# Hard-max attention: a group's key chosen in five steps, and the next batch's key differences formed on GpSimd in eight pieces

## The chip, the cores and the metric

One core of one Trainium2 chip. The time is that of one execution on the device, in microseconds (us); a run that is called *fast* is one of the undisturbed state, and only fast runs of the same rounds are compared. The profile was taken of one execution of each kernel. Its engines are PE (TensorE), PEld (weight loads), DVE (VectorE), ACT (ScalarE), POOL (GpSimd) and SP (the queue that issues most stores).

## The reference

```python
B, Sq, Sk, D = 4, 4096, 4096, 128           # q, k, v: float32, random normal
logits = np.matmul(q, k.transpose(0, 2, 1))
best = np.argmax(logits, axis=-1)
return v[b_idx, best, :]                    # the value row of the best key, for each query
```

The output needs the exact best key of each query, but not the logits.

## The kernel before

There are 128 iterations, 32 for each batch; an iteration handles 128 queries. The kernel screens in fp16 and repairs with exact arithmetic the few rows where the screen could be wrong.

1. *Screen.* Keys are taken in groups of four. TensorE and ScalarE give, per group, an upper figure of its four logits, 1024 figures per query. VectorE folds them into a word (`fold`: figure in the upper half, group number counted down in the lower half) and MAX8 takes the best eight words (`top`).
2. *Pick within the group.* `gather` cuts the group number out of the best word, and GpSimd fetches the group's three key differences k1-k0, k2-k0, k3-k0 with an indirect DMA. `dots` multiplies them with the query and adds up on VectorE; every two iterations make one such set. `pick`, once for each chunk of eight iterations (four at the end, 18 chunks in all), takes the best of the four and counts how many keys are near it. A second indirect DMA on GpSimd fetches the value row.
3. *Next batch.* Keys and queries of the next batch are loaded by GpSimd-issued DMAs (iterations 2 to 17 of a batch), and `put_k` forms the key differences on VectorE, two operations per batch, and stores them to DRAM, where the gathers of the next batch read them.
4. *Flags.* Rows whose decision is close are computed exactly: once in the middle of the kernel, beside the rest, and once at the end.

```python
def put_k(b, h):                                   # iterations 9 and 13 of the batch before
    src = natk[b % 2][:, h].rearrange("p (g f) d -> p g f d", f=4)
    nc.vector.tensor_tensor(out=kd[:, h], in0=src[:, :, 1:4, :],
                            in1=src[:, :, 0:1, :].to_broadcast([P, 4, 3, P]), op=OP.subtract)
    nc.sync.dma_start(out=kb16[:, h], in_=kd[:, h]...)
# ...
def dots(c, x, m):                                 # m = 2 iterations' queries
    yield "until", lambda: ("kg", x) in done, 2    # two iterations after the gathers were issued
    nc.vector.tensor_tensor(out=prod, in0=kg, in1=natq..., op=OP.mult)         # 128x768 fp16
    nc.vector.tensor_tensor(out=p1, in0=prod[..., 0:64], in1=prod[..., 64:128], op=OP.add)
    nc.vector.tensor_tensor(out=p2, in0=p1[..., 0:32], in1=p1[..., 32:64], op=OP.add)
    nc.vector.tensor_reduce(out=d[...], in_=p2, axis=AX_X, op=OP.add)

def pick(c, t0, t1):                               # seven VectorE operations; d is 128 x n x 4
    mx   = max over the four of d
    near = (d + NEAR) >= mx
    CNT  = sum of near                             # over 1.5: the row is flagged
    lt   = d < mx
    sel  = lt * 2**20 + iotab[b]                   # iotab: 0..3, plus the batch's first row
    wi   = min of sel
    win  = 4 * cand + wi                           # the row of v
    for j in range(n):                             # later, one or two per iteration
        late_q.append(lambda: nc.gpsimd.indirect_dma_start(out=vr[:, j, :], in_=v_flat, in_offset=win[:, j]))
# ... the loop, cut to its order:
for it in range(T):
    load_part(...)                                 # GpSimd issues a DMA, iterations 2..17 of a batch
    screen(it); fold(it - 1)
    if it % NQT in (9, 13): put_k(it // NQT + 1, it % NQT // 13)
    step(it)                                       # one operation of dots, pick, flags
    top(it - 2); gathers(it - 3); step(it)
    issue(it)                                      # GpSimd: one key gather, one or two value gathers
```

(The operations of `pick` are written as formulas here; `...` marks cuts.) GpSimd executes in the order of the program, so where an operation stands among its gathers decides when it runs.

Of the kernel before, what the change touches and what calls it, by code (L numbers as in the profile page):

```python
# [7 lines left out]
FP32 = mybir.dt.float32  # L8
FP16 = mybir.dt.float16
BF16 = mybir.dt.bfloat16  # L10
U32 = mybir.dt.uint32
# [3 lines left out]
AX_X = mybir.AxisListType.X  # L15
OP = mybir.AluOpType
AF = mybir.ActivationFunctionType
IOA = bass.IndirectOffsetOnAxis
# [9 lines left out]
def kernel(ctx, tc, q, k, v, out):  # L28
    nc = tc.nc
    B, Sq, D = q.shape  # L30
    Sk = k.shape[1]
    P = 128
    NQT = Sq // P
    T = B * NQT
    NG = Sk // 4

    k4 = k.rearrange("b (g f) d -> (b g) (f d)", f=4)
    v_flat = v.rearrange("b s d -> (b s) d")
# [14 lines left out]
    rec = dr.tile([P * T, 8], U32, name="rec")  # L53
    k16 = [dr.tile([NG, 384], FP16, name=f"k16_{b}") for b in range(B)]
    kT = [bp.tile([P, Sk], FP16, name=f"kT{i}", tag=f"kT{i}") for i in range(2)]
# [12 lines left out]
    def put_k(b, h):  # L68
        if b >= B:
            return  # L70
        src = natk[b % 2][:, h].rearrange("p (g f) d -> p g f d", f=4)
        nc.vector.tensor_tensor(out=kd[:, h], in0=src[:, :, 1:4, :], in1=src[:, :, 0:1, :].to_broadcast([P, 4, 3, P]),
                                op=OP.subtract)
        kb16 = k16[b].rearrange("(h p n) d -> p h (n d)", p=P, n=4)
        nc.sync.dma_start(out=kb16[:, h], in_=kd[:, h].rearrange("p g f d -> p (g f d)"))

    def load_part(b, i):
# [32 lines left out]
    for W in W_t:  # L110
        nc.gpsimd.iota(out=W.bitcast(U16)[:, 0::2].rearrange("p (h m r) -> p h m r", h=2, m=4),
                       pattern=[[-NG // 2, 2], [-1, 4], [-4, P]], base=NG - 1, channel_multiplier=0)

# [5 lines left out]

    iotab = [iota(f"iotab{b}", 4, b * Sk) for b in range(B)]  # L120
    iota4 = iotab[0]
    iota_r = iota("iota_r", P, 1)
# [111 lines left out]
    def gather(c, t0, n):  # L234
        c0, c1 = chunks[c]
        if t0 == c0:
            cand_t[c] = sp.tile([P, c1 - c0], U32, tag=f"cand{c1 - c0}", name=f"cand_{c}", bufs=3)
        x = cand_t[c][:, t0 - c0:t0 - c0 + n]
        nc.vector.tensor_scalar(out=x, in0=TOP.bitcast(U32)[:, t0:t0 + n, 0], scalar1=NG - 1, scalar2=NG - 1,
                                op0=OP.bitwise_and, op1=OP.bitwise_xor)  # L240
        kg = rp.tile([P, n, 3, P], FP16, tag=f"kg{n}", name=f"kg_{t0}", bufs=8)
        assert len(kg_t) < 8
        kg_t[t0] = kg
        for j in range(n):
            near_q.append(lambda j=j: nc.gpsimd.indirect_dma_start(  # L245
                out=kg[:, j].rearrange("p f d -> p (f d)"), out_offset=None, in_=k16[t0 // NQT],
                in_offset=IOA(ap=x[:, j:j + 1], axis=0)))
        mark = lambda: done.add(("kg", t0))
        marks.add(mark)
        near_q.append(mark)  # L250
        start(dots(c, t0, n), "dots", c)
# [20 lines left out]
    def pick(c, t0, t1):  # L272
        n = t1 - t0
        b, qt = t0 // NQT, t0 % NQT
        d = D_t[c % 3][:, 0:n, :]
        yield "until", lambda: all(("dot", x) in done for x in range(t0, t1, 2)), 0
        cand = cand_t.pop(c)
        mx = sp.tile([P, n, 1], FP32, tag=f"mx{n}", name=f"mx_{c}")
        nc.vector.tensor_reduce(out=mx[:, :, 0], in_=d, axis=AX_X, op=OP.max)
        yield "dve",  # L280
        near = sp.tile([P, n, 4], FP32, tag=f"near{n}", name=f"near_{c}")
        nc.vector.scalar_tensor_tensor(out=near, in0=d, scalar=NEAR, in1=mx.to_broadcast([P, n, 4]),
                                       op0=OP.add, op1=OP.is_ge)
        yield "dve",
        nc.vector.tensor_reduce(out=CNT[:, t0:t1], in_=near, axis=AX_X, op=OP.add)
        done.add(("cnt", c))
        yield "cnt",
        lt = sp.tile([P, n, 4], FP32, tag=f"lt{n}", name=f"lt_{c}")
        nc.vector.tensor_tensor(out=lt, in0=d, in1=mx.to_broadcast([P, n, 4]), op=OP.is_lt)
        yield "dve",  # L290
        sel = sp.tile([P, n, 4], FP32, tag=f"sel{n}", name=f"sel_{c}")
        nc.vector.scalar_tensor_tensor(out=sel, in0=lt, scalar=float(1 << 20),
                                       in1=iotab[b].unsqueeze(1).to_broadcast([P, n, 4]), op0=OP.mult, op1=OP.add)
        yield "dve",
        wi = sp.tile([P, n], FP32, tag=f"wi{n}", name=f"wi_{c}")
        nc.vector.tensor_reduce(out=wi, in_=sel, axis=AX_X, op=OP.min)
        yield "dve",
        win = sp.tile([P, n], U32, tag=f"win{n}", name=f"win_{c}")
        nc.vector.scalar_tensor_tensor(out=win, in0=cand, scalar=4.0, in1=wi, op0=OP.mult, op1=OP.add)
        vr = rp.tile([P, n, P], FP32, tag=f"vr{n}", name=f"vr_{c}", bufs=3 if n == 8 else 4)  # L300
        for j in range(n):
            late_q.append(lambda j=j: nc.gpsimd.indirect_dma_start(out=vr[:, j, :], out_offset=None, in_=v_flat,  # L302
                                                                   in_offset=IOA(ap=win[:, j:j + 1], axis=0)))

        def store():
            nc.sync.dma_start(out=out[b].rearrange("(p t) d -> p t d", p=P)[:, qt:qt + n], in_=vr)
            done.add(("out", c))

        stores.add(store)
        late_q.append(store)  # L310
# [6 lines left out]
    def flag_segment(t0, t1, ready, stored):  # L317
# [8 lines left out]
        yield "dve", 0.17  # L326
        nc.vector.scalar_tensor_tensor(out=F, in0=CNT[:, t0:t1], scalar=1.5, in1=F, op0=OP.is_gt, op1=OP.max)
        yield "dve", 0.17
# [81 lines left out]
        def get(dst, src, idx, hi):  # L410
# [6 lines left out]
        bo = fp.tile([P, 1], U32, tag="bo", name=f"bo_{t0}")  # L417
        nc.vector.tensor_scalar(out=bo, in0=row, scalar1=Sq.bit_length() - 1, scalar2=NG.bit_length() - 1,
                                op0=OP.logical_shift_right, op1=OP.logical_shift_left)
        yield "dve", 0.17  # L420
        gi = fp.tile([P, 3], U32, tag="gi", name=f"gi_{t0}")
        nc.vector.tensor_scalar(out=gi, in0=FR[:, 0:3], scalar1=NG - 1, scalar2=NG - 1, op0=OP.bitwise_and, op1=OP.bitwise_xor)
        yield "dve", 0.17
# [3 lines left out]
        for r in range(3):  # L427
            get(FK[:, r, :], k4, gb[:, r:r + 1], B * NG)
        yield "until", lambda: not fast, 3
# [17 lines left out]
    def flags_last(t0, t1, win_last, late):  # L447
        S = t1 - t0
        H, F = LF["H"], LF["F"]
        nc.vector.scalar_tensor_tensor(out=F, in0=CNT[:, t0:t1], scalar=1.5, in1=F, op0=OP.is_gt, op1=OP.max)  # L450
        Ec = fp.tile([P, S], FP32, tag="Ec", name="Ec_e")
# [41 lines left out]
        def get(dst, src, idx, hi):  # L493
# [7 lines left out]
        bo = fp.tile([P, 1], U32, tag="bo", name="bo_e")  # L501
        nc.vector.tensor_scalar(out=bo, in0=row, scalar1=Sq.bit_length() - 1, scalar2=NG.bit_length() - 1,
                                op0=OP.logical_shift_right, op1=OP.logical_shift_left)
# [4 lines left out]
        gi = fp.tile([P, 3], U32, tag="gi", name="gi_e")  # L508
        nc.vector.tensor_scalar(out=gi, in0=FR[:, 0:3], scalar1=NG - 1, scalar2=NG - 1, op0=OP.bitwise_and, op1=OP.bitwise_xor)
        gb = fp.tile([P, 3], U32, tag="gb", name="gb_e")  # L510
        nc.vector.tensor_tensor(out=gb, in0=gi, in1=bo.to_broadcast([P, 3]), op=OP.add)
        for r in range(3):
            get(FK[:, r, :], k4, gb[:, r:r + 1], B * NG)
        tot = fp.tile([P, 3], FP32, tag="tot", name="tot_e")
# [18 lines left out]
    def exact(kk, qq, grp, R, name):  # L533
        d = fp.tile([P, R, 4], FP32, tag=f"xd{R}", name=f"xd_{name}")
        for r in range(R):
            for f in range(4):
# [4 lines left out]
        ix = fp.tile([P, R, 4], FP32, tag=f"xi{R}", name=f"xi_{name}")  # L541
        nc.vector.scalar_tensor_tensor(out=ix, in0=grp.unsqueeze(2).to_broadcast([P, R, 4]), scalar=4.0,
                                       in1=iota4.unsqueeze(1).to_broadcast([P, R, 4]), op0=OP.mult, op1=OP.add)
        yield "dve", 0.17
# [22 lines left out]
    def all_rows():  # L567
# [4 lines left out]
        with tc.If(left > 0):  # L572
            for b in range(B):
                with tc.For_i(0, NQT, 1) as t:
# [4 lines left out]
                    g8 = fp.tile([P, 8], U32, tag="ag", name=f"ag_{b}")  # L579
                    nc.vector.tensor_scalar(out=g8, in0=w8, scalar1=NG - 1, scalar2=(NG - 1) | (b * NG),  # L580
                                            op0=OP.bitwise_and, op1=OP.bitwise_xor)
                    kk = fp.tile([P, 8, 512], FP32, tag="ak", name=f"ak_{b}")
                    for r in range(8):
                        nc.gpsimd.indirect_dma_start(out=kk[:, r, :], out_offset=None, in_=k4,
                                                     in_offset=IOA(ap=g8[:, r:r + 1], axis=0))
# [92 lines left out]
    for it in range(T):  # L678
# [17 lines left out]
        if it >= 1:  # L696
            fold(it - 1)
        if it % NQT in (9, 13):
            put_k(it // NQT + 1, it % NQT // 13)
        step(it)  # L700
        if it >= 2:
            top(it - 2)
        if it >= 3:
            gathers(it - 3)
        step(it)
        issue(it)

# [71 lines left out]
```

## Time and profile before

| | before |
|---|---|
| time | 474.54 us (474.13 to 474.59, 4 runs) |
| VectorE busy | 417.8 us of 472.4 |
| ScalarE, TensorE busy | 380.7, 381.7 us |
| GpSimd busy | 305.6 us |
| one iteration on VectorE | about 3.0 us |

The profile page of the kernel before: busy time of each engine, and the rows of VectorE and GpSimd in 40 slices of the span (a digit is the busy share in tenths).

```profile
PE 381.7 (81%) x1840; PEld 168.9 (36%) x1840; DVE 417.8 (88%) x845; ACT 380.7 (81%) x438; POOL 305.6 (65%) x345
...
DVE  4288999999999999999999999999999999998400
...
POOL 9025544666787876666878765667777567777740
```

VectorE has no free tenth between the start-up and the end. GpSimd seems to have a third left over.

The groups of instructions of the kernel before that the change touches. A line holds: place in the program, engine, operation, what it writes and reads, shapes, number; then busy us in all and the mean ns of one; then idle time before them and what ended it.

```profile
L302 POOL DMA_INDIRECT vr<-in_v_dram,win x128 | 125.5, 980 | 39.0 <-issue 35.0 <-DMA vr<-in_v_dram,win 0.9 <-DVE prod L260 0.6
L260 DVE TENSOR_TENSOR prod<-kg,natq 128x768 f16<-128x768 f16 x64 | 35.0, 549 | 1.5 <-DMA kg<-k,cand 1.5
L239 DVE TENSOR_SCALAR cand<-TOP 128x2 uint32<-128x2 uint32 x64 | 10.5, 164 | 0.0
L72 DVE TENSOR_TENSOR kd<-natk 128x1536 f16<-128x1536 f16 x8 | 7.7, 964 | 2.5 <-DMA natk<-in_k_dram 2.5
L296 DVE TENSOR_REDUCE wi<-sel 128x8 f32<-128x32 f32 x14 | 2.5, 178 | 0.0
L289 DVE TENSOR_TENSOR lt<-D,mx 128x32 f32<-128x32 f32 x14 | 2.4, 174 | 0.0
L494 POOL DMA_INDIRECT FV<-in_v_dram,xw_fe x1 | 1.0, 1004 | 0.8 <-DVE hi L569 0.8
```

A product of differences and queries takes 0.55 us, a key-difference operation 0.96 us, each step of the pick about 0.17 us by itself. The first line's mean of 0.98 us holds some longer ones; most value gathers take 0.94 us. The last line is a gather of the same table with a bounds check.

The timeline of GpSimd in the kernel before, in the second batch, while the third one loads. Columns: start, duration, engine, line, operation, number, and the idle time before it.

```profile
126.88 0.95 POOL L302 DMA_INDIRECT vr<-in_v_dram,win  x1 [0.30 <-issue]
127.83 0.61 POOL L63 DMA_DIRECT2D natk<-in_k_dram  x1
128.74 0.97 POOL L245 DMA_INDIRECT kg<-k,cand  x1 [0.30 <-DVE p L264]
130.02 0.94 POOL L302 DMA_INDIRECT vr<-in_v_dram,win  x1 [0.30 <-DMA kg<-k,cand]
130.96 0.61 POOL L63 DMA_DIRECT2D natk<-in_k_dram  x1
```

A gather is preceded by 0.30 us in which the profile counts GpSimd as not busy and shows nothing else on it. From one load to the next it is 3.13 us (130.96 - 127.83), which is more than VectorE's iteration of about 3.0 us. Here GpSimd has no third left over: it has nothing. (In the first batch it has room: 26.0 of the 49.5 us between iterations 8 and 24 are busy.)

The timeline of VectorE in the kernel before, in the first batch:

```profile
46.12 1.30 DVE L224 SCALAR_TENSOR_TENSOR W<-psn,E 128x1024 int16<-128x1024 f32 x1
47.31 0.55 DVE L260 TENSOR_TENSOR prod<-kg,natq 128x768 f16<-128x768 f16 x1
47.77 1.23 DVE L228 MAX8 TOP<-W 128x8 f32<-128x1024 f32 x1
48.91 0.15 DVE L239 TENSOR_SCALAR cand<-TOP 128x2 uint32<-128x2 uint32 x1
```

Fold, product, MAX8 and the cut of the group number stand end to end. Consecutive operations overlap by about 0.1 us; what an operation costs is its distance to the next start, 0.46 us for the product.

The waits of VectorE for gathered keys in the kernel before (total us, times, longest):

```profile
DVE prod L260 <- DMA kg<-k,cand: 1.5, 2, 1.0
```

### The profile page before, as it was taken

What the parts mean: (1) busy time and instruction counts of PE and PEld (TensorE: products, weight loads), DVE (VectorE), ACT (ScalarE), POOL (GpSimd) and SP (SyncE); (2) the same over time, 40 slices, a digit from 0 to 9 for tenths busy, and PEclk for the clock granted to TensorE, in tenths of its full rate; (3) what the DMA queues carried; (4) which work ended last, traced back from release to release, by engine and by line L of the source; (5) the groups of instructions that cost most, each with busy time, mean ns of one, the idle gap of its engine ahead of it and who ended that gap; (6) DMA issues with size and microseconds to landing.
All of it is one profiled execution on the core that took longest, in us unless ns stands there. A gap on an engine that the chain in (4) does not pass through costs nothing. (4 is left out here: it accounts for less than half of the span.)

```text
span 472.4 us, 6274 instructions
## 1 busy us (share of the span) xinstructions
PE 381.7 (81%) x1840; PEld 168.9 (36%) x1840; DVE 417.8 (88%) x845; ACT 380.7 (81%) x438; POOL 305.6 (65%) x345
## 2 busy tenths in 40 slices
PE   7899999999898889999888979999999889920000
PEld 4444444443343334443333434443333333300000
DVE  4288999999999999999999999999999999998400
ACT  1999999999998899999998889999999888920000
POOL 9025544666787876666878765667777567777740
PEclk9999999999999999999999999999999999975555
DMA  7914564143455946242666736142333132324320
GB/s 134 211 32 87 108 115 93 56 119 63 119 94 125 193 87 147 57 124 65 134 133 156 113 108 97 55 114 65 118 89 109 52 94 58 110 73 121 98 82 5
DMA packets 40777, 47.43 MB, mean 100 GB/s; under 512 B 24200, under 2 KB 32395, under 8 KB 40736
## 3 DMA queue, kind: packets, MB, share of 16 engines
q0 software_dynamic: 18464, 30.97, 31.1%
q1 hardware_dynamic: 22272, 16.00, 12.8%
q8 instruction: 15, 0.25, 0.2%
q14 instruction: 26, 0.21, 0.2%
HBM read 39.59 MB, written 12.19 MB: 110 GB/s over the span
## 5 line engine op out<-in xcount | busy, mean ns | idle before, releaser
L198 ACT ACTIVATE A<-pd 128x1024 f16<-128x1024 f32 x256 | 259.1, 1046 | 18.3 <-PE pd L189 17.8
L245 POOL DMA_INDIRECT kg<-k,cand x128 | 127.2, 994 | 103.9 <-DVE p L264 25.0
L224 DVE SCALAR_TENSOR_TENSOR W<-psn,E 128x1024 int16<-128x1024 f32 x128 | 166.4, 1300 | 15.1 <-ACT E L211 12.1
L189 PE MATMUL pd<-kT,qT 128*128 128x512 f16 x512 | 152.1, 378 | 17.4 <-ACT A L198 15.5
L189 PE MATMUL psn<-kT,qT 128*128 128x512 f16 x512 | 151.8, 377 | 15.4 <-ACT A L198 10.8
L189 PEld LDWEIGHTS <-qT 128*128 128x128 f16 x1024 | 98.4, 97 | 166.1 <-issue 77.9
L228 DVE MAX8 TOP<-W 128x8 f32<-128x1024 f32 x128 | 156.2, 1220 | 0.0
L208 PE MATMUL psn<-A,identh 128*128 128x512 f16 x512 | 152.0, 378 | 0.0
L302 POOL DMA_INDIRECT vr<-in_v_dram,win x128 | 125.5, 980 | 39.0 <-issue 35.0
L211 ACT ACTIVATE E<-psn 128x1024 int16<-128x1024 f32 x128 | 132.8, 1038 | 6.7 <-PE psn L208 5.9
L208 PEld LDWEIGHTS <-identh 128*128 128x128 f16 x512 | 49.5, 97 | 60.8
L260 DVE TENSOR_TENSOR prod<-kg,natq 128x768 f16<-128x768 f16 x64 | 35.0, 549 | 1.5 <-DMA kg<-k,cand 1.5
L264 DVE TENSOR_TENSOR p<-prod 128x384 f16<-128x384 f16 x64 | 22.3, 350 | 0.0
L269 DVE TENSOR_REDUCE D<-p 128x6 f32<-128x192 f16 x64 | 21.4, 338 | 0.0
L167 ACT ACTIVATE kT<-uk 128x256 f16<-128x256 f32 x48 | 20.0, 416 | 0.9 <-PE uk L164 0.9
L163 PE MATMUL uk<-identh,natk 128*128 128x128 f16 x96 | 15.8, 218 | 0.6 <-ACT A L198 0.6
L63 POOL DMA_DIRECT2D natk<-in_k_dram x26 | 15.7, 604 | 0.9 <-POOLq L763 0.8
L267 DVE TENSOR_TENSOR p<-p 128x192 f16<-128x192 f16 x64 | 15.7, 247 | 0.0
L66 POOL DMA_DIRECT2D natq<-in_q_dram x26 | 15.4, 594 | 0.1
L460 PE MATMUL fp_e<-n_e,tri 128*128 128x1 f32 x2 | 0.6, 362 | 16.4 <-DVE n_e L458 16.4
L164 PEld LDWEIGHTS <-natk 128*128 128x128 f16 x96 | 9.3, 97 | 7.7 <-issue 5.5
L163 PEld LDWEIGHTS <-natk 128*128 128x128 f16 x96 | 9.3, 97 | 5.6
(148 smaller groups left out, 142.4 us busy)
## 6 DMA issues: line engine op xcount, KB each, us to landing
out_dram<-vr SPq DMA_DIRECT2D x14, 512.0 KB, 3.2
k<-kd SPq DMA_DIRECT2D x8, 384.0 KB, 4.5
natk<-in_k_dram POOLq DMA_DIRECT2D x24, 128.0 KB, 3.8
natq<-in_q_dram POOLq DMA_DIRECT2D x24, 128.0 KB, 3.3
kg<-k,cand POOLq DMA_INDIRECT x128, 2.7
vr<-in_v_dram,win POOLq DMA_INDIRECT x128, 2.5
natk<-in_k_dram POOLq DMA_DIRECT2D x2, 512.0 KB, 7.0
out_dram<-vr SPq DMA_DIRECT2D x4, 256.0 KB, 2.3
```

The costliest lines, as they stand in the source:

```text
L163: nc.tensor.matmul(out=o, lhsT=natk[b % 2][:, h, 4 * m + x, :], rhs=identh, start=True, stop=False)
L189: nc.tensor.matmul(out=ps[:, n * 512:(n + 1) * 512], lhsT=qT[b % 2][:, qt * P:(qt + 1) * P], rhs=kT[b % 2][:, u * 1024 + n * 512:u * 1024 ...
L198: nc.scalar.activation(out=A, in_=ps, func=AF.Abs)
L208: nc.tensor.matmul(out=ps[:, n * 512:(n + 1) * 512], lhsT=identh, rhs=A[:, n * 512:(n + 1) * 512], start=False, stop=True)
L211: nc.scalar.activation(out=E, in_=ps, func=AF.Relu, scale=QSCALE)
L224: nc.vector.scalar_tensor_tensor(out=W_t[t % NW].bitcast(I16)[:, 1::2], in0=ps, scalar=QSCALE, in1=E, op0=OP.mult, op1=OP.max)
L228: nc.vector.max(out=TOP[:, t, :], in_=W_t[t % NW].bitcast(FP32))
L245: near_q.append(lambda j=j: nc.gpsimd.indirect_dma_start(out=kg[:, j].rearrange("p f d -> p (f d)"), out_offset=None, in_=k16[t0 // NQT], ...
L260: nc.vector.tensor_tensor(out=prod, in0=kg, in1=natq[b % 2][:, x - b * NQT:x - b * NQT + m, :].unsqueeze(2).to_broadcast([P, m, 3, P]), op ...
L264: nc.vector.tensor_tensor(out=p1, in0=prod[:, :, :, 0:64], in1=prod[:, :, :, 64:128], op=OP.add)
L269: nc.vector.tensor_reduce(out=d[:, x - c0:x - c0 + m, 1:4], in_=p2, axis=AX_X, op=OP.add)
L302: late_q.append(lambda j=j: nc.gpsimd.indirect_dma_start(out=vr[:, j, :], out_offset=None, in_=v_flat, in_offset=IOA(ap=win[:, j:j + 1], a ...
```

## The change

The intent is to take work off the engine that has no slack. (a) If each near key adds 8 plus its place in the group instead of 1, one sum tells both: exactly one near key gives 8 to 11, two or more give 17 or more (the row is now flagged above 12). Then `lt`, `wi` and one form of `sel` are not needed. An index from two near keys may pass the end of v, so the value gather gets a bounds check; such a row is flagged and repaired anyway. (b) The six differences of batches 1 to 3 go to GpSimd, in 24 pieces. The index is now carried as 4 times the group number; that changes constants and the shapes by which the tables are addressed.

```diff
+    def put_part(b, i):
+        h, g = i // 4, i % 4
+        x = natk[b % 2][:, h, 4 * g:4 * g + 4]
+        nc.gpsimd.tensor_tensor(out=kd[:, h, g], in0=x[:, 1:4, :], in1=x[:, 0:1, :].to_broadcast([P, 3, P]), op=OP.subtract)
+        if g == 3:
+            nc.sync.dma_start(out=k16[b]..., in_=kd[:, h]...)
...
-        nc.vector.tensor_reduce(out=CNT[:, t0:t1], in_=near, axis=AX_X, op=OP.add)
+        nc.vector.tensor_tensor(out=sel, in0=near, in1=iota8.unsqueeze(1).to_broadcast([P, n, 4]), op=OP.mult)
+        nc.vector.tensor_reduce(out=CNT[:, t0:t1], in_=sel, axis=AX_X, op=OP.add)
-        (lt, sel, wi, win: four operations)
+        nc.vector.scalar_tensor_tensor(out=win, in0=CNT[:, t0:t1], scalar=float(b * Sk - 8), in1=cand, op0=OP.add, op1=OP.add)
             late_q.append(lambda j=j: nc.gpsimd.indirect_dma_start(out=vr[:, j, :], ...,
-                                                                   in_offset=IOA(ap=win[:, j:j + 1], axis=0)))
+                                                                   in_offset=IOA(ap=win[:, j:j + 1], axis=0),
+                                                                   bounds_check=B * Sk - 1, oob_is_err=False))
...
-        if it % NQT in (9, 13):
-            put_k(it // NQT + 1, it % NQT // 13)
         step(it)
         ...
         step(it)
+        if 8 <= qt < 24 and qt % 2 == 0:
+            put_part(b + 1, (qt - 8) // 2)
         issue(it)
```

More of the change, by code (lines that the diff above doesn't have):

```diff
@@ L35 @@
     NG = Sk // 4
-    k4 = k.rearrange("b (g f) d -> (b g) (f d)", f=4)
+    IDX = 4 * (NG - 1)
+    k_flat = k.rearrange("b s d -> (b s) d")
     v_flat = v.rearrange("b s d -> (b s) d")
@@ L53 @@
     rec = dr.tile([P * T, 8], U32, name="rec")
-    k16 = [dr.tile([NG, 384], FP16, name=f"k16_{b}") for b in range(B)]
+    k16 = [dr.tile([Sk, 96], FP16, name=f"k16_{b}") for b in range(B)]
     kT = [bp.tile([P, Sk], FP16, name=f"kT{i}", tag=f"kT{i}") for i in range(2)]
@@ L73, in put_k @@
                                 op=OP.subtract)
-        kb16 = k16[b].rearrange("(h p n) d -> p h (n d)", p=P, n=4)
+        kb16 = k16[b].rearrange("(h p n) d -> p h (n d)", p=P, n=16)
         nc.sync.dma_start(out=kb16[:, h], in_=kd[:, h].rearrange("p g f d -> p (g f d)"))
+    def put_part(b, i):
+        if b >= B:
+            return
+        h, g = i // 4, i % 4
+        x = natk[b % 2][:, h, 4 * g:4 * g + 4]
+        nc.gpsimd.tensor_tensor(out=kd[:, h, g], in0=x[:, 1:4, :], in1=x[:, 0:1, :].to_broadcast([P, 3, P]), op=OP.subtract)
+        if g == 3:
+            nc.sync.dma_start(out=k16[b].rearrange("(h p n) d -> p h (n d)", p=P, n=16)[:, h],
+                              in_=kd[:, h].rearrange("p g f d -> p (g f d)"))
     def load_part(b, i):
@@ L111 @@
         nc.gpsimd.iota(out=W.bitcast(U16)[:, 0::2].rearrange("p (h m r) -> p h m r", h=2, m=4),
-                       pattern=[[-NG // 2, 2], [-1, 4], [-4, P]], base=NG - 1, channel_multiplier=0)
+                       pattern=[[-NG * 2, 2], [-4, 4], [-16, P]], base=IDX, channel_multiplier=0)
     def iota(name, n, base, mult=0):
@@ L118, in iota @@
         return x
-    iotab = [iota(f"iotab{b}", 4, b * Sk) for b in range(B)]
-    iota4 = iotab[0]
+    iota4 = iota("iota4", 4, 0)
+    iota8 = iota("iota8", 4, 8)
     iota_r = iota("iota_r", P, 1)
@@ L238, in gather @@
         x = cand_t[c][:, t0 - c0:t0 - c0 + n]
-        nc.vector.tensor_scalar(out=x, in0=TOP.bitcast(U32)[:, t0:t0 + n, 0], scalar1=NG - 1, scalar2=NG - 1,
+        nc.vector.tensor_scalar(out=x, in0=TOP.bitcast(U32)[:, t0:t0 + n, 0], scalar1=IDX, scalar2=IDX,
                                 op0=OP.bitwise_and, op1=OP.bitwise_xor)
@@ L284, in pick @@
         yield "dve",
-        nc.vector.tensor_reduce(out=CNT[:, t0:t1], in_=near, axis=AX_X, op=OP.add)
+        sel = sp.tile([P, n, 4], FP32, tag=f"sel{n}", name=f"sel_{c}")
+        nc.vector.tensor_tensor(out=sel, in0=near, in1=iota8.unsqueeze(1).to_broadcast([P, n, 4]), op=OP.mult)
+        yield "dve",
+        nc.vector.tensor_reduce(out=CNT[:, t0:t1], in_=sel, axis=AX_X, op=OP.add)
         done.add(("cnt", c))
         yield "cnt",
-        lt = sp.tile([P, n, 4], FP32, tag=f"lt{n}", name=f"lt_{c}")
-        nc.vector.tensor_tensor(out=lt, in0=d, in1=mx.to_broadcast([P, n, 4]), op=OP.is_lt)
-        yield "dve",
-        sel = sp.tile([P, n, 4], FP32, tag=f"sel{n}", name=f"sel_{c}")
-        nc.vector.scalar_tensor_tensor(out=sel, in0=lt, scalar=float(1 << 20),
-                                       in1=iotab[b].unsqueeze(1).to_broadcast([P, n, 4]), op0=OP.mult, op1=OP.add)
-        yield "dve",
-        wi = sp.tile([P, n], FP32, tag=f"wi{n}", name=f"wi_{c}")
-        nc.vector.tensor_reduce(out=wi, in_=sel, axis=AX_X, op=OP.min)
-        yield "dve",
         win = sp.tile([P, n], U32, tag=f"win{n}", name=f"win_{c}")
-        nc.vector.scalar_tensor_tensor(out=win, in0=cand, scalar=4.0, in1=wi, op0=OP.mult, op1=OP.add)
+        nc.vector.scalar_tensor_tensor(out=win, in0=CNT[:, t0:t1], scalar=float(b * Sk - 8), in1=cand, op0=OP.add, op1=OP.add)
         vr = rp.tile([P, n, P], FP32, tag=f"vr{n}", name=f"vr_{c}", bufs=3 if n == 8 else 4)
@@ L326, in flag_segment @@
         yield "dve", 0.17
-        nc.vector.scalar_tensor_tensor(out=F, in0=CNT[:, t0:t1], scalar=1.5, in1=F, op0=OP.is_gt, op1=OP.max)
+        nc.vector.scalar_tensor_tensor(out=F, in0=CNT[:, t0:t1], scalar=12.0, in1=F, op0=OP.is_gt, op1=OP.max)
         yield "dve", 0.17
@@ L417, in flag_segment @@
         bo = fp.tile([P, 1], U32, tag="bo", name=f"bo_{t0}")
-        nc.vector.tensor_scalar(out=bo, in0=row, scalar1=Sq.bit_length() - 1, scalar2=NG.bit_length() - 1,
+        nc.vector.tensor_scalar(out=bo, in0=row, scalar1=Sq.bit_length() - 1, scalar2=Sk.bit_length() - 1,
                                 op0=OP.logical_shift_right, op1=OP.logical_shift_left)
@@ L421, in flag_segment @@
         gi = fp.tile([P, 3], U32, tag="gi", name=f"gi_{t0}")
-        nc.vector.tensor_scalar(out=gi, in0=FR[:, 0:3], scalar1=NG - 1, scalar2=NG - 1, op0=OP.bitwise_and, op1=OP.bitwise_xor)
+        nc.vector.tensor_scalar(out=gi, in0=FR[:, 0:3], scalar1=IDX, scalar2=IDX, op0=OP.bitwise_and, op1=OP.bitwise_xor)
         yield "dve", 0.17
@@ L427, in flag_segment @@
         for r in range(3):
-            get(FK[:, r, :], k4, gb[:, r:r + 1], B * NG)
+            get(FK[:, r, :], k_flat, gb[:, r:r + 1], B * Sk)
         yield "until", lambda: not fast, 3
@@ L449, in flags_last @@
         H, F = LF["H"], LF["F"]
-        nc.vector.scalar_tensor_tensor(out=F, in0=CNT[:, t0:t1], scalar=1.5, in1=F, op0=OP.is_gt, op1=OP.max)
+        nc.vector.scalar_tensor_tensor(out=F, in0=CNT[:, t0:t1], scalar=12.0, in1=F, op0=OP.is_gt, op1=OP.max)
         Ec = fp.tile([P, S], FP32, tag="Ec", name="Ec_e")
@@ L501, in flags_last @@
         bo = fp.tile([P, 1], U32, tag="bo", name="bo_e")
-        nc.vector.tensor_scalar(out=bo, in0=row, scalar1=Sq.bit_length() - 1, scalar2=NG.bit_length() - 1,
+        nc.vector.tensor_scalar(out=bo, in0=row, scalar1=Sq.bit_length() - 1, scalar2=Sk.bit_length() - 1,
                                 op0=OP.logical_shift_right, op1=OP.logical_shift_left)
@@ L508, in flags_last @@
         gi = fp.tile([P, 3], U32, tag="gi", name="gi_e")
-        nc.vector.tensor_scalar(out=gi, in0=FR[:, 0:3], scalar1=NG - 1, scalar2=NG - 1, op0=OP.bitwise_and, op1=OP.bitwise_xor)
+        nc.vector.tensor_scalar(out=gi, in0=FR[:, 0:3], scalar1=IDX, scalar2=IDX, op0=OP.bitwise_and, op1=OP.bitwise_xor)
         gb = fp.tile([P, 3], U32, tag="gb", name="gb_e")
@@ L512, in flags_last @@
         for r in range(3):
-            get(FK[:, r, :], k4, gb[:, r:r + 1], B * NG)
+            get(FK[:, r, :], k_flat, gb[:, r:r + 1], B * Sk)
         tot = fp.tile([P, 3], FP32, tag="tot", name="tot_e")
@@ L541, in exact @@
         ix = fp.tile([P, R, 4], FP32, tag=f"xi{R}", name=f"xi_{name}")
-        nc.vector.scalar_tensor_tensor(out=ix, in0=grp.unsqueeze(2).to_broadcast([P, R, 4]), scalar=4.0,
-                                       in1=iota4.unsqueeze(1).to_broadcast([P, R, 4]), op0=OP.mult, op1=OP.add)
+        nc.vector.scalar_tensor_tensor(out=ix, in0=grp.unsqueeze(2).to_broadcast([P, R, 4]), scalar=0.0,
+                                       in1=iota4.unsqueeze(1).to_broadcast([P, R, 4]), op0=OP.add, op1=OP.add)
         yield "dve", 0.17
@@ L579, in all_rows @@
                     g8 = fp.tile([P, 8], U32, tag="ag", name=f"ag_{b}")
-                    nc.vector.tensor_scalar(out=g8, in0=w8, scalar1=NG - 1, scalar2=(NG - 1) | (b * NG),
+                    nc.vector.tensor_scalar(out=g8, in0=w8, scalar1=IDX, scalar2=IDX | (b * Sk),
                                             op0=OP.bitwise_and, op1=OP.bitwise_xor)
@@ L583, in all_rows @@
                     for r in range(8):
-                        nc.gpsimd.indirect_dma_start(out=kk[:, r, :], out_offset=None, in_=k4,
+                        nc.gpsimd.indirect_dma_start(out=kk[:, r, :], out_offset=None, in_=k_flat,
                                                      in_offset=IOA(ap=g8[:, r:r + 1], axis=0))
```

## The prediction

> **What bounds it now.** Between 40 and 400 us VectorE is busy 38.3 to 40.0 us of every 40 (busy time by stretch); TensorE and ScalarE are at 87 to 99%, the granted clock is 1.00. An iteration (one of 128) takes about 3.0 us of VectorE: fold 1.30, MAX8 1.22, the rest small. ScalarE is a close second: with nothing waiting (first seven iterations) its three activations repeat every 2.71 us; one with a key transpose takes 3.05, or 3.60 in stretches where TensorE and ScalarE wait for each other (timeline, ScalarE). GpSimd issues: a gather costs 0.94 us and 0.30 us before it, so two per iteration are 2.5 us; while the next batch loads (0.6 us each) it is 3.13 us per iteration, more than VectorE needs, and the gathers start up to 2.1 us late (timeline, 122 to 172 us). There gathered keys land only 2.2 to 2.8 us before their product starts, once too late (0.45 us). From about 397 us GpSimd runs back to back as well.
>
> **What the change does.**
> 1. Pick: seven VectorE operations become five, 18 times. Between independent work each costs 0.09 to 0.10 us from start to start (timeline), so 0.2 us per group: 3 us in all. In the last group the count comes one dependent operation (0.2 us) later.
> 2. Six of eight key-difference operations leave VectorE: 0.86 us from start to start, 5.2 us. Batch 0's two stay.
> 3. 24 GpSimd subtractions of 128x384 fp16. The Trainium skill, "GPSIMD Engine Reference", section 3.1, gives 4497 ns for 2048 fp32 elements; my estimate by proportion is 0.85 us, with dispatch about 1.0.
> 4. The value gathers get a bounds check. Gathers that have one take 1.00 us here, those without 0.94 (groups of instructions): +0.06 us, 128 times on GpSimd.
> 5. "SBUF — State Buffer", section "Who interferes with whom", says that a VectorE instruction with two SBUF inputs and a GpSimd instruction that reads SBUF exclude each other. Product, first and second add are such (about 1.15 us in 6). Where GpSimd keeps up, a piece falls mostly beside fold and MAX8; I allow 0.05 to 0.1 us per piece, 1.5 us in all.
>
> **On the critical path.** Batch 0's window (GpSimd has room): the full 1.7 us is gained. Batch 2's window (3.4 us per iteration with the flag work): about 1.5. Batch 1's: GpSimd would need 3.13 + 0.5 + 0.06 = 3.7 us per iteration for ten iterations, against 3.3 measured there; the lateness may grow by about 2.4 us before products wait. So nothing is gained there, up to 2 us may be lost. Picks: 2.5 of 3. Tail: GpSimd is the queue that ends it; some 20 checked gathers and the later count cost 1 to 1.5 us. Sum: -1.7 - 1.5 + 0.5 - 2.5 - 0.2 + 1 = about -4.4 us.
>
> **Prediction: 470.0 us, 465.5 to 474.5 in 8 of 10. Faster by over 2%: 0.08; within 2%: 0.91; slower: 0.01.**
>
> **What would show it.** VectorE busy falls by 8 to 10 us, the span by half. Six difference operations gone from VectorE; 24 on GpSimd near 1.0 us. Value gathers near 1.00 us. In batch 1's window (about 135 to 175 us) key gathers start over 4 us late and VectorE waits for gathered keys, several us in all (1.5 before). From the last MAX8 to the end: about 1 us longer.
>
> **What would make it wrong.** A GpSimd subtraction of 2 us or more: batches 1 and 2 wait, 474 or worse. One of 0.6 us with no exclusion: 466. ScalarE's 3.60 us rhythm kept because VectorE runs ahead: gains vanish into waits for ScalarE. Bounds check costing nothing: 1 to 2 us better.

## The result, and the profile after

| | before | after |
|---|---|---|
| time | 474.54 us (4 runs) | 480.41 us (480.23 to 482.42, 4 runs) |
| VectorE busy | 417.8 us | 417.6 us |
| GpSimd busy | 305.6 us | 338.2 us |

The ratio is 1.0135 (95% interval 1.0108 to 1.0163): slower by 1.3%, which is clear of the noise and within 2%. A ratio is always the mean time of one kernel's fast runs over that of the other's of the same rounds, so it is not quite the ratio of the medians quoted.

The same lines of the page of the kernel after:

```profile
PE 381.3 (80%) x1840; PEld 168.7 (35%) x1840; DVE 417.6 (87%) x803; ACT 380.9 (80%) x438; POOL 338.2 (71%) x367
...
DVE  4289999999999897999999999999999999996300
...
POOL 9026666766788888867788888757777777777730
```

VectorE executes 42 instructions fewer and is busy just as long. So others of its instructions must have become longer. The groups of instructions of the kernel after:

```profile
L306 POOL DMA_INDIRECT vr<-in_v_dram,win x128 | 134.4, 1050 | 39.0 <-issue 37.2 <-DMA vr<-in_v_dram,win 0.9 <-DVE rw_e L491 0.3
L271 DVE TENSOR_TENSOR prod<-kg,natq 128x768 f16<-128x768 f16 x64 | 39.5, 619 | 10.1 <-DMA kg<-k,cand 10.0
L83 POOL TENSOR_TENSOR kd<-natk 128x384 f16<-128x384 f16 x24 | 22.8, 950 | 0.2
L250 DVE TENSOR_SCALAR cand<-TOP 128x2 uint32<-128x2 uint32 x64 | 11.6, 181 | 0.0
L73 DVE TENSOR_TENSOR kd<-natk 128x1536 f16<-128x1536 f16 x2 | 1.9, 959 | 2.4 <-DMA natk<-in_k_dram 2.4
```

The pieces take 0.95 us each. The same 64 products take 4.5 us more in all (39.5 against 35.0), and VectorE waits 10.0 us for gathered keys instead of 1.5:

```profile
DVE prod L271 <- DMA kg<-k,cand: 10.0, 10, 2.1
```

Where the longer products are is seen by laying the timelines of two engines over each other. First VectorE, then GpSimd, in the kernel after, in the first batch:

```profile
45.06 1.29 DVE L235 SCALAR_TENSOR_TENSOR W<-psn,E 128x1024 int16<-128x1024 f32 x1
46.24 1.02 DVE L271 TENSOR_TENSOR prod<-kg,natq 128x768 f16<-128x768 f16 x1
47.19 1.22 DVE L239 MAX8 TOP<-W 128x8 f32<-128x1024 f32 x1
48.33 0.14 DVE L250 TENSOR_SCALAR cand<-TOP 128x2 uint32<-128x2 uint32 x1
```

```profile
44.30 1.00 POOL L256 DMA_INDIRECT kg<-k,cand  x1 [0.30 <-issue]
45.30 0.59 POOL L67 DMA_DIRECT2D natq<-in_q_dram  x1
45.87 0.97 POOL L83 TENSOR_TENSOR kd<-natk 128x384 f16<-128x384 f16 x1
```

The piece runs from 45.87 to 46.84. The fold, which started before it, is not affected (1.29 us). The product starts at 46.24, in the middle of the piece, and ends at 47.26, 0.42 us after the piece: it did most of its work only then. Its next start came after 0.95 us instead of 0.46. The second gather of an iteration pair, the load and the piece stand at a fixed distance behind the cut of the group number, and so does the product; the same meeting comes back at 52.59 (1.01 us), 58.92 (1.01) and 65.33 (0.93). All ten products of this run that met a piece ended 0.42 or 0.43 us after it, wherever in the piece they had started.

The same in the second batch, where GpSimd is behind. VectorE, then GpSimd, in the kernel after:

```profile
155.53 1.31 DVE L235 SCALAR_TENSOR_TENSOR W<-psn,E 128x1024 int16<-128x1024 f32 x1
157.75 1.20 DVE L271 TENSOR_TENSOR prod<-kg,natq 128x768 f16<-128x768 f16 x1 [0.91 <-DMA kg<-k,cand]
```

```profile
154.68 0.99 POOL L256 DMA_INDIRECT kg<-k,cand  x1 [0.30 <-issue]
155.97 1.01 POOL L306 DMA_INDIRECT vr<-in_v_dram,win  x1 [0.30 <-issue]
156.98 0.60 POOL L67 DMA_DIRECT2D natq<-in_q_dram  x1
157.58 0.95 POOL L83 TENSOR_TENSOR kd<-natk 128x384 f16<-128x384 f16 x1
```

The product waits for its keys, whose gather began at 154.68. They land about 3 us later, which is just when GpSimd has got to the piece (2.90 us after the gather's start). So a product that had waited 0.91 us for late keys was then held for most of a piece. It happens at 157.75, 165.32 and 172.72 alike (after waits of 0.91, 0.89 and 0.44 us).

Read by stage: start of the fold of an iteration, us, in the profiled runs.

| iteration | 8 | 24 | 40 | 56 | 72 | 88 | 127 | end of span |
|---|---|---|---|---|---|---|---|---|
| before | 42.5 | 92.0 | 140.2 | 192.3 | 240.9 | 296.3 | 419.1 | 472.4 |
| after | 42.3 | 93.0 | 140.8 | 197.4 | 245.2 | 301.3 | 423.0 | 478.5 |

The pieces stand in iterations 8 to 22, 40 to 54 and 72 to 86. Between 8 and 24 the kernel after takes 1.2 us longer (50.7 against 49.5), between 40 and 56 4.5 us longer, between 72 and 88 0.7 us longer, although in each 1.7 us of differences are gone from VectorE. Outside it gains a little everywhere. After the last fold it loses 2.2 us again (55.5 against 53.3). Of the 4.5 us of the second window, VectorE was busy for 1.0 and idle for 3.5 (busy 51.4 of 56.6 us, before 50.4 of 52.1).

### The profile page after: what moved, and what is told of

Its sections match the earlier page's. It is cut to its first block, busy times and chain, and to the rows that moved or that the text cites. A ratio compares the mean times of both kernels' runs of the same rounds, so it can differ in the third digit from the quotient of the medians.

```text
span 478.5 us, 6364 instructions
## 1 busy us (share of the span) xinstructions
PE 381.3 (80%) x1840; PEld 168.7 (35%) x1840; DVE 417.6 (87%) x803; ACT 380.9 (80%) x438; POOL 338.2 (71%) x367
## 5 line engine op out<-in xcount | busy, mean ns | idle before, releaser
L306 POOL DMA_INDIRECT vr<-in_v_dram,win x128 | 134.4, 1050 | 39.0 <-issue 37.2
L219 PEld LDWEIGHTS <-identh 128*128 128x128 f16 x512 | 49.5, 97 | 60.8
L271 DVE TENSOR_TENSOR prod<-kg,natq 128x768 f16<-128x768 f16 x64 | 39.5, 619 | 10.1 <-DMA kg<-k,cand 10.0
L83 POOL TENSOR_TENSOR kd<-natk 128x384 f16<-128x384 f16 x24 | 22.8, 950 | 0.2
L278 DVE TENSOR_TENSOR p<-p 128x192 f16<-128x192 f16 x64 | 16.7, 264 | 0.0
L175 PEld LDWEIGHTS <-natk 128*128 128x128 f16 x96 | 9.3, 97 | 8.9 <-issue 6.4
```

Of the source, the lines that this page charges most:

```text
L83: nc.gpsimd.tensor_tensor(out=kd[:, h, g], in0=x[:, 1:4, :], in1=x[:, 0:1, :].to_broadcast([P, 3, P]), op=OP.subtract)
L219: nc.tensor.matmul(out=ps[:, n * 512:(n + 1) * 512], lhsT=identh, rhs=A[:, n * 512:(n + 1) * 512], start=False, stop=True)
L271: nc.vector.tensor_tensor(out=prod, in0=kg, in1=natq[b % 2][:, x - b * NQT:x - b * NQT + m, :].unsqueeze(2).to_broadcast([P, m, 3, P]), op ...
L306: late_q.append(lambda j=j: nc.gpsimd.indirect_dma_start(out=vr[:, j, :], out_offset=None, in_=v_flat, in_offset=IOA(ap=win[:, j:j + 1], a ...
```

## The experiments

Theory A: the pieces are the loss, and it has two parts. A1: VectorE operations with two inputs in SBUF are held while GpSimd reads SBUF. The Trainium skill, "SBUF — State Buffer", section "Who interferes with whom", says so: such an instruction "contends with a GpSimd instruction that reads SBUF, not with one that only writes it". A2: GpSimd's queue becomes too long and keys come late. Rivals: B, the new pick or the check; C, pieces and checked gathers only together; D, the later store of the differences. All kernels gave correct results.

### One part at a time

**e1_pick_only.** The change with the differences back on VectorE.

```diff
+        if it % NQT in (9, 13):
+            put_k(it // NQT + 1, it % NQT // 13)
-        if 8 <= qt < 24 and qt % 2 == 0:
-            put_part(b + 1, (qt - 8) // 2)
```

> The change with its five-step pick and its bounds check, but the key differences back on VectorE in two operations per batch, as before. If the GpSimd pieces are the loss (theory A): the pick's 3 us less about 1.2 us for the checked gathers, 472.5 us (471.5 to 473.5). If the pick itself or the check is the loss (rival B): 477 us or more.

Measured: 471.71 us, ratio to before 0.9944 (0.9932 to 0.9957). The five-step pick is a gain, and B falls.

**e2_pick_unchecked.** The same, and `bounds_check=B * Sk - 1, oob_is_err=False` taken away.

> The same without the bounds check on the value gathers (no index is out of range on this draw). Theory A: the gathers fall back from 1.00 to 0.94 us and about 1.2 us are gained, 471.3 us. Rival B with the check as the loss: 4 us or more below the run with the check. If the check costs nothing in time: both alike.

Measured: 470.95 us, ratio 0.992 (0.9908 to 0.9933). Alone the check costs 0.8 us by the medians, though the intervals of the two ratios just overlap. The pick without it gains 3.6 us. In both runs the stretch from the last fold to the end is over a microsecond longer than before (54.5 and 55.1 us against 53.3), where GpSimd's gathers, one behind the other, end the kernel.

**e3_pieces_only.** The kernel before with `put_part` at its places instead of `put_k`.

> The kernel before with the 24 GpSimd pieces alone: old pick, no bounds check. Theory A: the pieces by themselves cost 6 to 8 us, about 481 us, although 5.2 us of VectorE work went. Rival C (the pieces would fit, and only together with the checked gathers is the GpSimd queue too long): 475 us or less.

Measured: 477.86 us (475.5 to 479.3), ratio 1.006 (1.0037 to 1.0084). The pieces alone make the kernel slower, but by 3.3 us, half of what was expected. The parts do not add up: -3.6 + 0.8 + 3.3 gives 475.0 and not 480.4. This stays open until the last runs.

**e4_pieces_vector.** The change with `nc.vector.tensor_tensor` in place of `nc.gpsimd.tensor_tensor` in `put_part`.

> The change with its eight pieces per batch at their places, but on VectorE (each about 0.26 us there, 6.3 us in all against 5.2 us in two operations). Theory A (it is GpSimd that makes the pieces dear): 473.5 us. Rival D (the later writing of the differences, and the store that holds up the other stores behind it, is the loss): 477 us or more.

Measured: 473.40 us, ratio 0.9979 (0.9966 to 0.9992). With eight pieces per batch at the same places and the same stores, but on VectorE, the kernel takes 1.7 us more than e1, for which the smaller cutting is enough (24 operations of 0.35 us against 6 of 0.95). D falls; it is GpSimd that makes them dear.

### Holding or queue

Both kernels leave all of VectorE's work as before and add 24 operations of about 1 us on GpSimd at the pieces' places. They differ in the instruction: the subtraction reads SBUF and writes it, the memset only writes.

**e5_dummy_read.** Before, plus

```diff
+            nc.gpsimd.tensor_tensor(out=scr, in0=x[:, 1:4, :], in1=x[:, 0:1, :].to_broadcast([P, 3, P]), op=OP.subtract)
```

> The kernel before, unchanged, plus the 24 GpSimd subtractions at the places of the change, written to a scratch tile that nobody reads: GpSimd's load of the change with nothing taken off VectorE. From the run of pieces alone (3.3 us slower although 5.2 us of VectorE work went) a piece costs about 0.35 us: 482 us (480 to 484).

**e6_dummy_write.** Before, plus

```diff
+            nc.gpsimd.memset(scr, 0.0)          # 128 x 1064 float32
```

> The kernel before plus 24 GpSimd memsets of about 0.95 us at the same places: the same time taken from GpSimd's queue, but nothing read from SBUF. Theory A1 (VectorE's operations with two SBUF inputs are held while GpSimd reads): products and adds keep their 0.55 and 0.35 us, and only late gathers remain: 475.5 to 477.5 us. Theory A2 (GpSimd's queue is too long, holding plays no part): within 1 us of the run with dummy reads, about 482.

Measured: reads 482.23 us, ratio 1.0161 (1.0149 to 1.0173); writes 475.14 us, ratio 1.001 (0.9995 to 1.0024). The groups, first of the run with reads, then of the run with writes:

```profile
L83 POOL TENSOR_TENSOR scr<-natk 128x384 f16<-128x384 f16 x24 | 24.2, 1010 | 0.2
```

```profile
L83 POOL MEMSET scr<- 128x1064 f32 x24 | 24.8, 1034 | 0.0
```

They take GpSimd's time alike. Now one meeting in each: VectorE and GpSimd in the run with reads, then in the run with writes.

```profile
66.27 0.92 DVE L268 TENSOR_TENSOR prod<-kg,natq 128x768 f16<-128x768 f16 x1
```

```profile
65.79 0.98 POOL L83 TENSOR_TENSOR scr<-natk 128x384 f16<-128x384 f16 x1
```

```profile
65.63 0.54 DVE L268 TENSOR_TENSOR prod<-kg,natq 128x768 f16<-128x768 f16 x1
```

```profile
65.11 1.05 POOL L83 MEMSET scr<- 128x1064 f32 x1
```

The second product starts inside the memset (65.11 to 66.16), ends with it (66.17) and keeps its 0.54 us. The first one starts inside the subtraction (65.79 to 66.77) and ends 0.42 us after it. So the queue's time by itself costs next to nothing (0.5 us) over the whole kernel before, and the reading costs 7.1 us, 0.30 us for a piece, with all that it sets off. A1 is shown, and its size on the kernel before.

A2 is not nothing, though. By stage (one profiled run of each), from iteration 40 to 56 the run with memsets takes 54.6 us against 52.1 before, and nearly all of the 2.5 us is idle time of VectorE; it regains more than half of that later. In the run with reads the three windows take 2.4, 3.1 and 2.7 us more than before. So in the second batch GpSimd's queue alone is enough for most of the loss, and in the first and third it is the reading.

### Other places for the pieces

**e7_after_issue.** The change, with the pieces one place later in GpSimd's order.

```diff
-        if 8 <= qt < 24 and qt % 2 == 0:
-            put_part(b + 1, (qt - 8) // 2)
         issue(it)
+        if 8 <= qt < 24 and qt % 2 == 0:
+            put_part(b + 1, (qt - 8) // 2)
```

> The change, each piece moved one place in GpSimd's order: behind the two gathers of the same iteration instead of ahead of them. Where GpSimd keeps up (batch 0) it then falls beside MAX8, the reduction and the fold and not beside the product. Theory A1 with a fixed phase: batch 0's window wins about 3 us, products there 0.55 us; batches 1 and 2 are still late: 476 us. If collisions come by chance, or holding plays no part: 480 as the change.

Measured: 480.15 us, ratio 1.0128 (1.0113 to 1.0142). A miss. In the first iterations there are no value gathers yet, and the piece now followed at once on the key gather, where it met the second add (0.97 to 0.99 us instead of 0.25, four times). From iteration 18 on, with a value gather ahead of it, it fell beside reduction and fold as meant. In the later batches, behind as they were, products were held up to 2.00 us. The longest one (159.63 to 161.63) had started 0.66 us before its piece (160.29 to 161.21), which stood directly behind a gather: a hold can begin before the piece is shown as running. Why is not known.

**e8_late.** As e7, in iterations 16 to 30 (`16 <= qt < 32`, `qt - 16`).

> As the last, and the pieces eight iterations later (16 to 30 of each batch instead of 8 to 22), mostly past the loads, so that GpSimd is not asked for more than it has. Theory A1+A2: the late gathers go as well, and most of the 5.2 us taken from VectorE is seen: 468 us (466.5 to 470). If a piece costs 0.3 us wherever it stands: 474 or more.

Measured: 473.90 us, ratio 0.9986 (0.9972 to 1.0001). Better than the change by 6.5 us, but a miss: in the first batch all but one piece fell beside MAX8, reduction and fold, and iteration 40 was reached at 138.7 us (140.2 before). In the second, pieces met the cut of the group number, which took 0.99 and 1.06 us instead of 0.15. With two gathers per iteration GpSimd has no room for a piece in every second one: 2 x 2 x 1.25 to 1.31 us and 1.08 for the piece are over 6 us, and two iterations take VectorE about 5.9.

### Eight runs on a disturbed chip

Four kernels were run twice, each time on a chip (two different ones) where the kernel before itself took 514 to 526 us, its clock taken down in stretches (mean granted clock 0.90 to 0.93 in these runs, 0.94 elsewhere).

**e9_unchecked** is the change without the check. **e10_pick_write** is e1 plus the memsets of e6, **e12_pick_read** e1 plus the subtractions of e5. **e11_first_batch** is the version described under e18 below. The second time they are called e13 to e16.

> The change without the bounds check. The parts do not add up: pick unchecked -3.6, pieces +3.3, check +0.8 would give 475.0, and 480.4 was measured. If the check's 0.06 us on 128 gathers makes GpSimd, already late because of the pieces, so late that products wait (theory E): 477 us or less. If the check costs its 0.8 us here as it did without pieces (rival F: it is the faster VectorE that meets the pieces and GpSimd's pace): 479 to 480 us.

> The five-step pick with its check and the differences on VectorE (471.7 us), plus 24 GpSimd memsets of about 0.95 us at the pieces' places, which read nothing. If holding by reads is the loss also with the shorter pick: 472 to 473.5 us. If with the shorter pick and the check GpSimd's queue is too long by itself: 476 us or more.

> The same with subtractions into a scratch tile in place of the memsets; it differs from the change only in that VectorE still forms the differences itself (5.2 us). Against the memsets, holding should cost about 7 us as it did on the kernel before: 479 to 480 us. If so, taking the differences from VectorE gained nothing in the change (480.4), because what ends a product's wait there is GpSimd. If parts add up instead, this run is 5 us above the change: 485.

> The version that the runs point to: five-step pick; no bounds check, because in the second half of the batches the sum counts down, so that a group with two near keys gives a smaller index and never one past the end; the pieces on GpSimd only for batch 1's keys, behind the two gathers of iterations 16 to 30 of batch 0, where they fell beside reductions and folds; the other differences on VectorE. 470.95 less about 0.9 us: 470.0 us (469 to 471). If it is 471 or more, GpSimd pieces gain nothing even there.

> The change without the bounds check, again on another chip. If the check's 0.06 us on 128 gathers makes GpSimd, already late because of the pieces, so late that products wait (theory E): 477 us or less. If the check costs only its 0.8 us here as it did without pieces (rival F: it is the faster VectorE that meets the pieces and GpSimd's pace): 479 to 480 us.

> Five-step pick with its check, differences on VectorE, plus 24 GpSimd memsets of about 0.95 us at the pieces' places, again on another chip. If holding by reads is the loss also with the shorter pick: 472 to 473.5 us. If with the shorter pick and the check GpSimd's queue is too long by itself: 476 us or more.

> The same with subtractions into a scratch tile in place of the memsets, again on another chip; it differs from the change only in that VectorE still forms the differences itself (5.2 us). Holding should cost about 7 us over the memsets: 479 to 480 us, and then taking the differences from VectorE gained nothing in the change (480.4). If parts add up: 485.

> Again on another chip: five-step pick, sum counting down in the second half so that no index passes the end and no check is needed, pieces on GpSimd for batch 1's keys alone, behind the gathers of iterations 16 to 30. 470.95 less about 0.9 us: 470.0 us (469 to 471). If 471 or more, GpSimd pieces gain nothing even there.

| | first time, ratio to before | second time |
|---|---|---|
| change without check | 0.9931 (0.9821 to 1.0041) | none (state mixed) |
| pick + memsets | 1.003 (0.9958 to 1.0102) | 1.0079 (1.0012 to 1.0147) |
| pick + subtractions | 1.0119 (1.004 to 1.0198) | 0.9925 (0.9842 to 1.0008) |
| e11_first_batch | 0.9867 (0.9807 to 0.9927) | 0.9769 (0.9668 to 0.987) |

Nothing is concluded from them: VectorE often waited for TensorE there (fold for `psn`, 26.9 us in e9, 3.0 in the kernel before), and the third row even changes its sign. Whether memsets and subtractions differ by the same 7 us when the pick is short is left open.

### The last two runs, undisturbed

**e17_unchecked.** The change, without the check:

```diff
-                                                                   in_offset=IOA(ap=win[:, j:j + 1], axis=0),
-                                                                   bounds_check=B * Sk - 1, oob_is_err=False))
+                                                                   in_offset=IOA(ap=win[:, j:j + 1], axis=0)))
```

> The change without the bounds check, for the third time, in the hope of an undisturbed chip. Theory E (the check makes late gathers later, products wait and meet the next piece): 477 us or less. Rival F (the check costs its 0.8 us and no more; it is the faster VectorE that meets pieces and pace): 479 to 480 us. On a disturbed chip nothing follows.

Measured: 475.90 us (473.0 to 477.35), ratio 1.0014 (0.9985 to 1.0043). Rival F falls: in the company of the pieces the check costs 4.5 us (480.41 - 475.90, in different rounds; the intervals of the two ratios lie far apart), and 0.8 us without them. The way that theory E names, later gathers, is not what the traces show: in the second batch key gathers start up to 5.79 us behind the cut of the group number here and 6.06 in the change, and that window is only 0.4 us shorter (56.2 us). The first and the third window and the tail are 1.1, 1.8 and 1.1 us shorter. In the first, the two cuts that met pieces took 0.81 us each in the change and 0.26 and 0.24 here. So for the most part the check seems to have moved the meetings; with one profiled run of each this is argued. What stays is close to the plain sum of pick and pieces (474.2). The runs of this kernel spread over 4 us, as those of e3 did, and those of e1 and e2 over 1.4: where pieces and products meet is a matter of tenths of a microsecond. That this is the reason for the spread is argued, not shown.

**e18_first_batch.** What the runs point to: pieces only where GpSimd has room and the meeting is harmless, and no check. In the second half of the batches the place in the group is counted down, so that a sum over two near keys gives a smaller row and never one past the end; in the first half a row that is too large is still a row of v.

```diff
+    iota8 = [iota("iota8", 4, 8), iota("iota8n", 4, -11)]
...  (sel takes iota8[b >= B // 2]; win adds 11 instead of -8 there)
-        nc.vector.scalar_tensor_tensor(out=F, in0=CNT[:, t0:t1], scalar=12.0, in1=F, op0=OP.is_gt, op1=OP.max)
+        nc.vector.scalar_tensor_tensor(out=F, in0=CNT[:, t0:t1], scalar=-12.0, in1=F, op0=OP.is_lt, op1=OP.max)
...
+        if it >= NQT and it % NQT in (9, 13):
+            put_k(it // NQT + 1, it % NQT // 13)
...      issue(it)
+        if 16 <= it < NQT and it % 2 == 0:
+            put_part(b + 1, (qt - 16) // 2)
```

> The version that the runs point to, for the third time. On an undisturbed chip 470.0 us (469 to 471), ratio 0.988 to 0.992. On a disturbed one its ratio was 0.987 and 0.977 with intervals of 1 to 2%; a ratio clearly above 0.99 there would contradict those.

Measured: 470.07 us (469.76 to 470.69), ratio to before 0.9913 (0.9898 to 0.9927). It beats both kernels, by 0.9% and 2.2% (470.07 against 474.35 of the same rounds, and against 480.41 of others). That 470.0 was expected is luck in its last digit: the runs spread over 0.9 us. And it is not shown that the eight pieces gain anything: e2, the same pick without a check or pieces, had 0.992 (0.9908 to 0.9933), and the intervals overlap. VectorE, then GpSimd, in the run of e18:

```profile
81.39 0.34 DVE L280 TENSOR_REDUCE D<-p 128x6 f32<-128x192 f16 x1
81.64 1.30 DVE L235 SCALAR_TENSOR_TENSOR W<-psn,E 128x1024 int16<-128x1024 f32 x1
82.83 0.55 DVE L271 TENSOR_TENSOR prod<-kg,natq 128x768 f16<-128x768 f16 x1
```

```profile
81.21 0.92 POOL L83 TENSOR_TENSOR kd<-natk 128x384 f16<-128x384 f16 x1
```

The piece lies beside a reduction (one input) and a fold (one input in SBUF, the other in PSUM), both at their usual length, and is over before the product starts. The first of the eight pieces (67.30) did hold an operation, a multiplication of the pick (0.81 us).

## Why the prediction was wrong

The prediction was 470.0 us, 465.5 to 474.5; measured was 480.41.

- **The step that failed** is the fifth, in its words: "Where GpSimd keeps up, a piece falls mostly beside fold and MAX8; I allow 0.05 to 0.1 us per piece, 1.5 us in all." The rule it took from the skill was right and is seen in the trace; the size was not. Reads against writes measured 7.1 us, 0.30 us per piece, on the kernel before. In the change, with each VectorE operation compared with its like in e1, those beside a piece are 8.9 us longer, 0.37 us per piece: 3.1, 3.2 and 2.7 us in the three batches. The pieces don't fall mostly beside fold and MAX8: in the first batch, the very place where GpSimd does keep up, four of eight fell where a product started, and two more on the cut of the group number, which the step did not count at all. And the 1.5 us are not carried into the sum, none of whose terms is this one.
- **By stage** the sum and the measurement compare so (before to after, windows from iteration 8 to 24 of a batch): first window -1.7 predicted, +1.2 measured; second +0.5, +4.5; third -1.5, +0.7; the tail +1, +2.2; all the rest, mostly picks, -2.7, -2.5. The three windows hold 9.1 of the 10.5 us between -4.4 and +6.1.
- **Batch 0, "the full 1.7 us is gained"**: follows from that step and falls with it. The window from iteration 8 to 24 became 1.2 us longer.
- **The check, "1 to 1.5 us" in the tail**: 0.8 us without pieces (e1 - e2), 4.5 us with them (480.41 - 475.90). The +0.06 us per gather was read rightly (0.94 and 1.00 us). That it would be paid several times over, it seems because it moves the meetings, was not seen. (This loss is in part the same as the holding: without the check the operations beside pieces are 5.5 us longer than in e2, not 8.9.)
- **Batch 1, "nothing is gained there, up to 2 us may be lost"**: the mechanism was right, the size was not. Key gathers started up to 6.06 us behind the cut of the group number there (2.17 before), and VectorE's waits for gathered keys rose from 1.5 to 10.0 us in the whole kernel, from 0.4 to 5.2 there. The loss was 4.5 us, and operations there were held for 3.2 us as well.
- **The pick, 2.5 us of 3**: right; 3.6 us with no check.
- **Durations**: right. A piece 0.95 us (1.0 predicted; the estimate by proportion from "GPSIMD Engine Reference", section 3.1, was 0.85), six operations gone from VectorE, 24 on GpSimd.
- **"VectorE busy falls by 8 to 10 us"**: wrong, it fell by 0.2 us. A held instruction counts as busy: 8.9 us of holding came in the place of what went. For that reason the busy share can't show this loss; the mean length of an unchanged instruction (product 549 to 619 ns) can.
- **The tail, "about 1 us longer"**: 2.2 us in the change, and over 1 us in e1 and e2 too.
- **"within 2%: 0.91"** came true by size alone: the forecast was a gain, the result a loss.

What is shown: that the pieces are the loss (e1, e4), that over the whole kernel before it is their reading and not their time (e5 against e6), and that check and pieces together cost more than apart (e17). How the loss in the change divides can be read from its trace beside e1's: VectorE's busy time is 4.0 us longer (8.9 of holding, less about 5.2 for the differences that went), its waits for gathered keys 7.0 us longer (10.0 against 3.0), its other waits a little shorter, the span 9.3 us longer. Not shown by a run of its own: how much of those waits holding itself caused, and whether reads against writes differ by as much with the short pick.

## What to carry to other kernels

Work that is moved from VectorE to GpSimd costs VectorE time again if, as here, it reads SBUF while VectorE has operations with two SBUF inputs; lay the timelines of both engines over each other and ask what the moved piece will stand beside, since in a periodic program it may stand there every time. Judge GpSimd's room by start-to-start distances, not by its busy share: at 65% busy this one had, in the loading stretch of the second batch, none. To tell holding from queueing, put an operation of the same length there that only writes.

## What the Trainium skill lacked or had wrong

- "SBUF — State Buffer", "Who interferes with whom": confirmed in both directions, reads 482.23 us against writes 475.14. It gives no duration for this pair: a product of 0.55 us that started inside a piece ended 0.42 or 0.43 us after the piece's end, whenever it had started, and so took 0.60 to 1.20 us in the change; 0.30 us per piece was lost on average (e5 against e6). A piece can be held too: 1.42 us instead of 0.97 behind a key-difference operation (e5, 144.14).
- The same section names `tensor_scalar` as one that can take the shared pair, under conditions. In these runs even one of two elements per partition, uint32, was held beside a reading piece (0.81 us in the change, up to 1.06 in e8, or 1.55 where a gather went before the piece, instead of 0.15). It was held without any reading piece as well: 1.17 us in e6, until the issue of a load ended (243.53).
- "Perfetto Trace Analysis" says, of moving work between the engines, that GpSimd and VectorE share an SBUF read port, "so offloading operations between those two might not help". Confirmed: the pieces alone cost 3.3 us (477.86 against 474.54). Neither that page nor "VectorE: DVE Perf Modes" was found to say that a held VectorE instruction is shown as busy: VectorE's busy time stayed at 417.6 us with 42 instructions fewer.
- No page was found that gives the cost of a bounds check on an indirect DMA: 1.00 us against 0.94 us on GpSimd.
- No page was found that gives the idle 0.30 us which the profile shows ahead of each gather, mostly 0.16 us behind a subtraction, and which GpSimd's busy share leaves out.
